# A two-block network on one core: a quarter of one MLP's up-projection matmuls walk their 512 columns in four other orders

## The chip, the cores and the metric

The kernel runs on one core of one Trainium2 chip. The metric is device time in microseconds of the whole program, from launch to end. The profile shows one execution of it, on five engines: TensorE (PE for matmuls, PEld for the loads of the stationary operand), VectorE (DVE), ScalarE (ACT), GpSimd (POOL) and SyncE (SP), beside the DMA queues.

## The reference, cut to what matters

The reference is a first block (a gated delta-net and retention mixer with a convolutional MLP) followed by a second block with two layers, each an attention and a relu-squared MLP. The change touches the MLP of the first of those two layers alone. Sizes: 512 tokens, model width 1024, hidden width 4096, all float32.

```python
def sq_relu_mlp(xn, w_in, w_out):
    h = jax.nn.relu(xn @ w_in)          # (512, 1024) @ (1024, 4096)
    return (h * h) @ w_out              # (512, 4096) @ (4096, 1024)

# in second_block, for i in range(2):
    h = h + mix
    h = h + sq_relu_mlp(rms_norm(h, norm_mlp_g[i]), mlp_w_in[i], mlp_w_out[i])
```

## The kernel before, in words

Everything is held feature-major: a tile has 128 features on the partitions and the 512 tokens as its columns. The normed activations of the MLP are eight such tiles, `st.x`, each as a pair: a rounded high part `xh` and the remainder `xl`, both of the type float32r (the trace prints their matmuls as f32). Weights come from HBM in the order of use, a block of 1024 x 256 at a time (line 243), and are split into `hi` and `lo` in the same way by ScalarE (line 251) and VectorE (line 252).

One output tile (128 hidden features x 512 tokens) is one call of `project` (line 381). It takes one bank of the accumulation memory (`ps`, 128 x 512 float32, tag `pj`, three buffers) and runs over the eight tiles of `st.x`; for each it issues three matmuls through `mm3` (line 190): hi by xh, hi by xl, lo by xh. So a tile of an up projection is 24 matmuls with 512 columns each, all adding into the same `ps`, each with its own load of 128 x 128 weights. All of them have line 188 in the profile (the helper `mm`), which is why they are told apart by their tiles: `ps_pj<-xh,hi`, `ps_pj<-xl,hi` and `ps_pj<-xh,lo`.

`mlp2(l, ...)` (line 962) is the relu-squared MLP of layer `l`. It goes through the hidden width in two halves. In each half a loop over eight weight blocks (`j`), two output tiles per block (`i`), calls `project`, then ScalarE takes relu out of `ps` into `s` (line 973), VectorE multiplies `ps` by `s` (line 974), and the product is split into `ah` (ScalarE, line 276) and `al` (VectorE, line 277). After sixteen tiles `out_proj` (line 440) multiplies them by the down weights: eight output tiles of 48 matmuls each, evacuated at lines 469 and 470. The order of the matmuls is the program's order; nothing is rescheduled by the change.

Elsewhere the kernel already reads and writes some tiles in other orders than the straight one, and the prediction uses these places:

- `cols_of` and `blocks` (lines 679 to 708): float32 matmuls whose moving operand is 64 columns in four runs of 16 (every other 16 of 128), written straight into `ps_X`, `ps_T` and `ps_U`.
- line 619: a matmul whose moving operand is two runs of 128 columns, 512 apart, written straight into `ps_gram`.
- `rev` (line 984): VectorE and ScalarE read `ps` backwards within each 128 columns, at lines 1383 and 1385 among others.
- `order`, `rorder` and `nat` (lines 1013 to 1028): for the second and third group of heads, line 1037 writes its output with a step of 128 or 32 elements between neighbours, and lines 1180 and 1252 read the accumulation memory in that way. For the first group, `order` is straight and `rorder` is `rev`.
- line 656: a VectorE copy out of a float32 tile with a step of 32 elements between neighbours.

## Time and profile before

| what | value |
|---|---|
| runs | 1921.4, 1927.18, 1923.35 us |
| median of the runs | 1923.35 us |
| the profiled execution, its own time | 1921.55 us |
| its span, first to last instruction | 1919.7 us |
| mean granted TensorE clock | 0.997 of full speed |
| busy | PE 98%, PEld 80%, DVE 58%, ACT 40%, POOL 7% |
| instructions on PE | 9219 matmuls, 9219 weight loads |
| chain that ended last, by engine | PE 55%, DVE 3%, ACT 1%, issue 1% |

[...] What a matmul costs in a stream is the distance from one start to the next, its pitch, and that is read from the timeline or from a long piece of the chain divided by its count.

### The profile page before, as it was taken

The page shows a single profiled execution, that of the slowest core. Times are in us where ns is not written, and L with a number is a line of the kernel's source. Part 1 is how long each engine was busy: PE and PEld are TensorE (multiplying, and loading weights), DVE is VectorE, ACT ScalarE, POOL GpSimd, SP SyncE. Part 2 cuts the span into 40 slices and gives each one's busy share as a digit, 9 for nine tenths or more (in the row PEclk, how much of TensorE's full clock was granted, in tenths as well). Part 3 has the DMA queues.
Part 4 walks back from the last instruction along what each step waited for, and adds up shares of the span by engine and source line. Part 5 has one row for each costly group of instructions (what it writes and reads, how often), then busy time and mean ns, then how long its engine had stood idle before and what let it go on. Part 6 is the DMA issues. An engine that isn't in the chain of part 4 may idle for free.

```text
span 1919.7 us, 23518 instructions
## 1 busy us (share of the span) xinstructions
PE 1885.3 (98%) x9219; PEld 1545.1 (80%) x9219; DVE 1109.8 (58%) x2109; ACT 766.1 (40%) x1350; POOL 143.3 (7%) x136
## 2 busy tenths in 40 slices
PE   7999999999999999999999999999999999999997
PEld 5887878788888887777888888888888888888886
DVE  7795756666356575558544344447877754334433
ACT  5523334343234444345342133336656543213322
POOL 1231210011001002000000000001111000000000
PEclk9999999999999999999999999999999999999999
DMA  5231213222322234112323222333222232222321
GB/s 191 79 116 56 74 45 121 95 88 88 110 103 86 76 112 160 64 52 99 110 89 109 88 106 92 111 131 135 95 73 101 81 112 88 97 101 89 109 88 44
DMA packets 39646, 185.53 MB, mean 97 GB/s; under 512 B 9055, under 2 KB 10847, under 8 KB 22000
## 3 DMA queue, kind: packets, MB, share of 16 engines
q1 hardware_dynamic: 37552, 177.45, 26.3%
q0 software_dynamic: 1984, 6.59, 1.0%
q8 instruction: 72, 1.18, 0.2%
q14 instruction: 38, 0.31, 0.1%
HBM read 176.31 MB, written 7.71 MB: 96 GB/s over the span
## 4 chain that ended last, share of the span: by engine, by line
PE 55%; DVE 3%; ACT 1%; issue 1%; DVEq 0%; ACTq 0%
PE ps_pj L188 49%; PE ps_ob L188 1%; PE ps_lgb L188 1%; PE ps_po L188 1%; PE ps_aT L1380 1%; PE ps_lg L188 1%; ACT junk L1397 0%; PE ps_bc L188 0%; DVE KL L1337 0%; DVE lo L252 0%; DVE nb L408 0%; DVE nb L409 0%; PE ps_obT L1409 0%; PE ps_pT L1140 0%; PE ps_mean L188 0%
## 5 line engine op out<-in xcount | busy, mean ns | idle before, releaser
L188 PE MATMUL ps_pj<-xh,hi 128*128 128x512 f32 x1504 | 592.2, 394 | 10.2 <-ACT hi L251 9.3
L188 PE MATMUL ps_pj<-xl,hi 128*128 128x512 f32 x1504 | 591.7, 393 | 0.0
L188 PE MATMUL ps_pj<-xh,lo 128*128 128x512 f32 x1504 | 590.9, 393 | 0.0
L251 ACT ACTIVATE hi<-raw 128x1024 fp32r<-128x1024 f32 (+2 forms) x308 | 317.2, 1031 | 649.1 <-PE ps_pj L188 611.0
L252 DVE TENSOR_TENSOR lo<-raw,hi 128x1024 fp32r<-128x1024 f32 (+2 forms) x308 | 369.6, 1202 | 300.2 <-ACT hi L251 299.2
L188 PEld LDWEIGHTS ps_pj<-xh,hi 128*128 128x128 f32 x1504 | 283.1, 188 | 69.0 <-ACT hi L251 9.8
L188 PEld LDWEIGHTS ps_pj<-xh,lo 128*128 128x128 f32 x1504 | 283.1, 188 | 58.1 <-DVE lo L252 1.1
L188 PEld LDWEIGHTS ps_pj<-xl,hi 128*128 128x128 f32 x1504 | 283.1, 188 | 57.6 <-DVE xl L280 0.6
L188 PE MATMUL ps_pj<-ah,lo 128*128 128x512 f32 (+1 forms) x704 | 271.0, 385 | 0.0
L188 PE MATMUL ps_pj<-al,hi 128*128 128x512 f32 (+1 forms) x704 | 270.7, 385 | 0.2 <-DVE al L277 0.2
L188 PE MATMUL ps_pj<-ah,hi 128*128 128x512 f32 (+1 forms) x704 | 270.9, 385 | 0.0
L188 PEld LDWEIGHTS ps_pj<-al,hi 128*128 128x128 f32 x704 | 132.3, 188 | 26.9 <-DVE al L277 0.5
L188 PEld LDWEIGHTS ps_pj<-ah,hi 128*128 128x128 f32 x704 | 132.3, 188 | 26.4 <-ACT ah L276 0.4
L188 PEld LDWEIGHTS ps_pj<-ah,lo 128*128 128x128 f32 x704 | 132.3, 188 | 25.9
L469 DVE TENSOR_TENSOR ot<-ps_pj,r 128x512 f32<-128x512 f32 x31 | 21.5, 692 | 108.1 <-PE ps_pj L188 108.1
L188 PE MATMUL ps_pj<-mh,hi 128*128 128x512 f32 x192 | 74.9, 394 | 1.0 <-ACT mh L276 0.9
L276 ACT ACTIVATE ah<-ms 128x512 fp32r<-128x512 f32 x64 | 40.4, 632 | 87.4 <-DVE ms L974 85.9
L188 PE MATMUL ps_pj<-ml,hi 128*128 128x512 f32 x192 | 74.4, 392 | 0.6 <-DVE ml L277 0.6
L188 PE MATMUL ps_pj<-mh,lo 128*128 128x512 f32 x192 | 74.0, 390 | 0.0
L277 DVE TENSOR_TENSOR al<-ms,ah 128x512 fp32r<-128x512 f32 x64 | 44.3, 693 | 45.0 <-ACT ah L276 45.0
L947 DVE SCALAR_TENSOR_TENSOR my<-ms,cols,my 128x511 f32<-128x511 f32 (+1 forms) x88 | 65.6, 748 | 2.8 <-ACT my L945 1.3
L1364 ACT ACTIVATE Lb<-Lb,bmn 128x512 f32<-128x512 f32 x64 | 45.6, 714 | 13.9 <-DVE bmn L1362 11.6
(341 smaller groups left out, 1895.9 us busy)
## 6 DMA issues: line engine op xcount, KB each, us to landing
raw<-w_all SPq DMA_DIRECT2D x137, 1024.0 KB
bt<-biasd SPq DMA_DIRECT2D x16, 448.0 KB
raw<-w_all SPq DMA_DIRECT2D x8, 768.0 KB
raw<-w_all SPq DMA_DIRECT2D x8, 640.0 KB
hscr<-h POOLq DMA_DIRECT2D x16, 256.0 KB, 2.5
hold<-hscr SPq DMA_DIRECT2D x16, 256.0 KB
hs<-x_t SPq DMA_DIRECT2D x8, 256.0 KB
hold<-x_t SPq DMA_DIRECT2D x8, 256.0 KB
```

The source lines that it names most:

```text
L188: return nc.tensor.matmul(o, lhsT=l, rhs=r, start=start, stop=stop)
L251: act(out=hv, in_=iv, func=AF.Copy)
L252: i_lo = V.tensor_tensor(out=lv, in0=iv, in1=hv.bitcast(F32), op=ALU.subtract)
L276: act(out=dst_hi, in_=src, func=AF.Copy)
L277: V.tensor_tensor(out=dst_lo, in0=src, in1=dst_hi.bitcast(F32), op=ALU.subtract)
L469: V.tensor_tensor(out=t, in0=ps, in1=scale_row, op=ALU.mult)
L947: V.scalar_tensor_tensor(out=y[:, jj:], in0=s[:, :T - jj], scalar=col(base + m), in1=y[:, jj:], op0=ALU.mult, op1=ALU.add)
L1364: act(out=L, in_=L, func=AF.Exp, scale=-1.0, bias=mn[:, j, t:t + 1], accum_out=ss[:, j, t:t + 1])
L1380: nc.tensor.transpose(ps[:, t * P:(t + 1) * P], A[t][:, kt * P:(kt + 1) * P], ident)
```

## The change

A table `VIEWS` names four pairs of weight blocks of the first relu-squared MLP (layer 0). For the tiles of these blocks `project` hands the matmul the same moving tiles and the same output tile, both seen through a view that lists the 512 columns in another order:

- half 0, blocks 2 and 3: columns 511 down to 0.
- half 0, blocks 6 and 7: 16 columns of the first 256, then 16 of the second 256, and so on (0 to 15, 256 to 271, 16 to 31, ...).
- half 1, blocks 2 and 3: the same with runs of 8.
- half 1, blocks 6 and 7: the same with runs of 2.

Moving operand and output use the same view, so each token's sum lands in the column where it landed before. Weights, order of the matmuls, their count and everything that reads `ps` afterwards stay as they are. Two blocks are four tiles, so each view covers 4 x 24 = 96 matmuls, 384 in all.

```diff
+VIEWS = {
+    (0, 0, 1): lambda ap: bass.AP(ap.tensor, ap.offset + T - 1, [list(ap.ap[0]), [-1, T]]),
+    (0, 0, 3): lambda ap: ap.rearrange("p (a i c) -> p i a c", a=2, c=16),
+    (0, 1, 1): lambda ap: ap.rearrange("p (a i c) -> p i a c", a=2, c=8),
+    (0, 1, 3): lambda ap: ap.rearrange("p (a i c) -> p i a c", a=2, c=2),
+}
@@ project
-    def project(pieces, x, n=T, cols=P):
+    def project(pieces, x, n=T, cols=P, view=None):
...
         nk = len(x)
+        if view is not None:
+            for k in range(nk):
+                hi, lo = pieces[k // KD]
+                M_["pe"] = mm3(view(ps), (hi[:, k % KD, 0:cols], lo[:, k % KD, 0:cols]),
+                               (view(x[k][0]), view(x[k][1])), k == 0, k == nk - 1)
+            return ps
@@ mlp2
-                        ps = project(w[i:i + 1], st.x)
+                        ps = project(w[i:i + 1], st.x, view=VIEWS.get((l, half, j // 2)))
```

## Rows read from the trace of the kernel before

**Rows 1.** The page: span, busy time by engine, granted clock in 40 slices.
```profile
span 1919.7 us, 23518 instructions
PE 1885.3 (98%) x9219; PEld 1545.1 (80%) x9219; DVE 1109.8 (58%) x2109; ACT 766.1 (40%) x1350; POOL 143.3 (7%) x136
PEclk9999999999999999999999999999999999999999
```
**Rows 2.** Chain that ended last, 940 to 1300 us: start, us, what.
```profile
944.06 1.16 PE ps_bc L188 x8
945.22 346.36 PE ps_pj L188 x1528
1291.58 0.95 PE ps_mean L188 x8
```
**Rows 3.** Stretches of the first relu-squared MLP: length, engines' busy (instructions), clock, DMA.
```profile
1030.00:1117.00 87.00, 87.00 (x386) 72.03 (x385) 30.47 (x33) 16.98 (x16) 0.00 (x0) 1.00 0.27 95
1117.00:1204.00 87.00, 87.00 (x386) 72.03 (x385) 39.72 (x48) 34.83 (x48) 0.00 (x0) 1.00 0.28 98
```
**Rows 4.** Waits, 943 to 1293 us: who waited for whom, us, times, longest.
```profile
ACT hi L251 <- PE ps_pj L188: 182.5, 62, 4.4
ACT ah L276 <- DVE ms L974: 43.7, 31, 1.4
```
**Rows 5.** Timeline of PE, one up tile with 512 columns: start, us, engine, line.
```profile
995.62 0.39 PE L188 MATMUL ps_pj<-xh,hi 128*128 128x512 f32 x1
...
1000.83 0.39 PE L188 MATMUL ps_pj<-xh,lo 128*128 128x512 f32 x1
```
**Rows 6.** Timeline of PE, last down tile, matmuls with 256 columns.
```profile
1895.77 0.28 PE L188 MATMUL ps_pj<-ah,hi 128*128 128x256 f32 x1
...
1898.65 0.28 PE L188 MATMUL ps_pj<-ah,hi 128*128 128x256 f32 x1
```
**Rows 7.** Groups by line and form: TensorE with two runs, with one, on 256 columns.
```profile
L188 PE MATMUL ps_gram<-KQ,kT x32: 379/379/564, 67.4 to 208.9; 128*128 128x256 f32 x32
L188 PE MATMUL ps_sT<-rqk 128*128 128x256 f32 x8 | 2.4, 379 | 0.0
```
**Rows 8.** Group (us, mean ns) and timeline: matmuls in runs of 16; of one column.
```profile
L188 PE MATMUL ps_X<-T,N 128*128 128x64 f32 x32 | 4.2, 275 | 0.7 <-POOL T L671 0.7
145.44 1.00 PE L188 MATMUL ps_X<-T,N 128*128 128x64 f32 x8
1291.51 1.02 PE L188 MATMUL ps_mean<-inv_d,acc 128*128 128x1 f32 x8
```
**Rows 9.** Other engines reading PSUM: straight, backwards, stepped (min/median/max or mean, ns).
```profile
L1443 DVE COPY bs<-ps_bias 16x512 f32<-16x512 f32 x3 | 2.0, 679 | 0.9 <-PE ps_bias L188 0.9
L1385 DVE COPY aT<-ps_aT 128x512 f32<-128x512 f32 x16 | 10.6, 683 | 0.8 <-PE ps_aT L1380 0.4 <-issue 0.2
L1180 DVE COPY L<-ps_bc x3: 681/681/694, 873.8 to 875.0; 128x512 f32<-128x512 f32 x3
L743 DVE COPY U<-ps_U 64x256 f32<-64x256 f32 x4 | 1.7, 417 | 4.6 <-PE ps_U L188 4.5
L430 ACT ACTIVATE rs<-ps_bc x5: 597/599/600, 30.6 to 1560.9; 128x512 f32<-128x512 f32 x5
L1252 ACT ACTIVATE oT<-ps_po x4: 598/598/599, 763.3 to 814.4; 128x512 f32<-128x512 f32 x4
L656 DVE COPY tt<-tt x2: 370/718/1066, 126.0 to 234.2; 64x256 f32<-64x256 f32 x2
```
**Rows 10.** Timeline of DVE, line 1037: backward, stepped, straight, stepped writes.
```profile
754.19 0.69 DVE L1037 TENSOR_TENSOR q<-ps_pj,rs 128x512 f32<-128x512 f32 x1 [1.60 <-PE ps_pj L188]
759.64 1.09 DVE L1037 TENSOR_TENSOR q<-ps_pj,rs 128x512 f32<-128x512 f32 x1 [4.75 <-PE ps_pj L188]
771.12 0.69 DVE L1037 TENSOR_TENSOR k<-ps_pj,rs 128x512 f32<-128x512 f32 x1 [6.69 <-PE ps_pj L188]
776.56 1.07 DVE L1037 TENSOR_TENSOR k<-ps_pj,rs 128x512 f32<-128x512 f32 x1 [4.75 <-PE ps_pj L188]
```

## The prediction

> **What bounds the kernel now.** I read the page first: TensorE is busy for 1885.3 of 1919.7 us and its granted clock stands at the top of the scale in all 40 slices [rows 1]. Then I looked for the place that the change touches, the first relu-squared MLP, in the chain of work that ended last. From 945.22 us on the chain is one unbroken piece of TensorE, 1528 matmuls in 346.36 us, which is 346.36 / 1528 = 226.7 ns per matmul [rows 2]; the MLP has 2 x (16 x 24 + 8 x 48) = 1536, so the piece is the whole of it but for the first few. The table by stretch says the same from the other side: in 87 us TensorE is busy for 87.00 us at a granted clock of 1.00, VectorE for 30 to 40 and ScalarE for 17 to 35 [rows 3]. The waits of that stretch are those of the others: ScalarE waited 182.5 us for TensorE to release weight buffers and 43.7 us for VectorE's squares [rows 4]; no wait of a matmul of the MLP is among them. So in this stage each nanosecond by which a matmul's pitch changes reaches the end of the program undiminished, and nothing else in the stage can give it back.

> **What a column costs.** The pitch has to be taken apart, because the change touches the columns only. With 512 columns 23 pitches take 1000.83 - 995.62 = 5.21 us, 226.5 ns each [rows 5]. The last down tile runs the same three products on 256 columns: 24 pitches in 1898.65 - 1895.77 = 2.88 us, 120.0 ns each [rows 6]. [...]

> **The change, part by part.** It removes and adds no instruction: 384 matmuls keep their place, their weights and their count of columns. No DMA, no wait and no queue moves. The readers of the output tile (relu on ScalarE, product on VectorE) read it straight as before, so their cost is nil on any account; if the matmuls of a tile became slower, those two would only wait longer for them, and the weight splits, which wait for TensorE now, have more time still. The one unknown is the pitch of 4 x 96 matmuls. Straight orders go to a new place in memory one column after the other. The new ones differ in two things: a step of -1, and jumps between the halves, 512 / 16 = 32, 512 / 8 = 64 and 512 / 2 = 256 of them per matmul.

> Jumps on TensorE: the trace has two kinds of matmul with a moving operand in pieces. Two runs of 128 take 379 ns, and a straight operand of 256 columns takes 379 ns too [rows 7]: one jump costs nothing that can be seen. Eight matmuls with four runs of 16 span 1.00 us, the last of them 275 ns, and eight with one column each 1.02 us [rows 8]; these are bound by their weight loads, so they say only that runs of 16 do no harm large enough to stick out behind those, (1.00 - 0.275) / 7, about 104 ns for 64 columns. That leaves room for half rate and more, so it does not prove the point at 0.416 ns per column.

> Backwards and stepped on the other engines: VectorE reads PSUM straight in 679 ns, backwards in 683, and with a step between all neighbours in no more than 694; ScalarE needs 599 straight and at most 599 stepped [rows 9]. A VectorE copy that reads SBUF with a step of 32 elements needs 370 ns for 256 elements in the better of its two records, while a straight one of 256 out of PSUM takes 417 [rows 9] (the other record, 1066, lies in a stage with much else going on). Writing SBUF backwards costs VectorE nothing either, 0.69 us against 0.69. Writing it with a step of 128 does: 1.09 us and 1.07 against 0.69 [rows 10], that is 0.40 us / 512 = 0.78 ns per element on top of (683 - 417) / 256 = 1.04 ns [rows 9], a factor of 1.75. This is the only row in which an order costs anything, and there every element jumps. In the change no column stands alone: each new order keeps neighbouring pairs together, the runs of 2 too.

> So the cost has these bounds. Below: the 13.5 ns per matmul could at the very most vanish, 384 x 13.5 = 5.2 us faster. Above, for one view: the stepped write's factor 1.75, which I round up to half rate: 512 x 0.416 = 213 ns per matmul, 96 x 213 = 20.4 us. For all four, 384 x 213 = 81.8 us. I take zero, because the reads in the trace are free in every order, and because the nearest TensorE row, the two runs, is free as well. Sum: 1921.55 us for the profiled execution, plus 0. The median of the runs shown lies 1.8 us above that execution; I put the forecast between the two, at **1922.5 us**. A measurement of this kernel can tell about 0.3%, 5.8 us, from no change.

> [...] No row here shows a matmul that writes its output out of order.

> **The rivals.**

> 1. The jumps cost, so that the time is longer: on the moving side each run opens a new place in SBUF, and the shorter the run, the less there is to hide that behind. A jump at VectorE's stepped-write price [rows 10] gives 32 x 0.78 = 25 ns, 64 x 0.78 = 50 ns and 256 x 0.78 = 200 ns per matmul; times 96: 2.4 + 4.8 + 19.2 = 26.4 us. At one column period per jump it is 1.3 + 2.6 + 10.2 = 14.1 us. If only the runs of 2 fall to half rate it is 20.4 us. So 1937 to 1949 us. It decides from 5.8 us / (96 x 352 jumps) = 0.17 ns per jump on. For it: TensorE asks for a run of 2 every 0.83 ns, faster than any engine in the trace, and stepped writes pay. Against it: stepped reads don't pay at one element per 1.04 ns, and the two runs didn't.

> 2. The backward order alone costs: if TensorE pairs neighbours only when they ascend, its 96 matmuls fall to half rate, +20.4 us, 1943 us. For it: 0.416 ns per column is 2.5 times VectorE's rate, so something may handle two at once. Against it: backward reads and writes at 683 and 0.69, as straight [rows 9, 10].

> 3. Every order that isn't one ascending run halves the rate, on the output side: +81.8 us, 2004 us. For it: nothing in the trace, which has no such output. Against it: the runs of 16 are 32 straight pieces, and reads of PSUM in any order are free [rows 9]. [...]

> 4. The change does not do what it says: a view in two dimensions could be issued as two matmuls of 256 columns. Then the pitch is 2 x 120.0 = 240 instead of 226.5, and even on all 384 that is 5.2 us, inside what can't be told from no change; the count of matmuls would show it.

> [...]

> **How the numbers follow.** No cost: 0.57. Split into two: 0.02. Jumps cost: 0.20. Backwards alone: 0.10. All at half rate: 0.09. Faster: 0.02. So within 0.3%: 0.57 + 0.02 = 0.59; slower: 0.20 + 0.10 + 0.09 = 0.39; faster: 0.02. The range reaches from 1918, the forecast less most of what the fixed part could give, to 1949, the upper end of the first rival, and takes in the second. It leaves out the third, and with it about 1 in 10.

> **What the profile of the changed kernel would show.** If I am right, the chain still has one TensorE piece of about 346 us there, and the timeline shows a pitch of 226 to 227 ns in all four places: about 961 to 983 us (backwards), 1005 to 1027 (runs of 16), 1135 to 1157 (runs of 8) and 1179 to 1201 (runs of 2). Under the first rival the pitch rises from one view to the next with the count of runs, with the runs of 2 at 330 to 440 ns; under the second only the first place changes, to 440 ns; under the third all four read about 440. A tile's span in the first place, 24 pitches, tells it at a glance: 5.4 us or 10.5 (24 x 0.4395). If all four pitches stay and the time still moves, the step that failed is that nothing else is touched.

## The result: 0.7% slower, and the whole of it in the pitch of the four places

| | before | changed |
|---|---|---|
| median of 6 runs | 1923.34 us | 1936.98 us |
| lowest to highest | 1921.4 to 1929.89 | 1935.74 to 1944.41 |
| ratio, 95% interval | | 1.0069 [1.0049, 1.0089] |
| the profiled execution, span | 1919.7 us | 1940.9 us |

The forecast was no change, 1922.5 us; the time lies 14.5 us above it, inside the range but clearly on the slower side. The page of the changed kernel and the piece of its chain that answers to [rows 2] (start, us, what):

```profile
span 1940.9 us, 23528 instructions
PE 1904.6 (98%) x9219; PEld 1549.8 (80%) x9219; DVE 1109.5 (57%) x2109; ACT 766.1 (39%) x1350; POOL 143.4 (7%) x136
...
950.81 1.16 PE ps_bc L197 x8
951.97 360.85 PE ps_pj L197 x1528
1312.83 0.88 PE ps_mean L197 x8
```

The piece has the same 1528 matmuls as in [rows 2] and takes 360.85 us in place of 346.36: 14.49 us more, which is the loss of the medians (13.6 us) to within a microsecond. It begins 6.75 us later than before, 951.97 against 945.22, and that has nothing to do with the change, whose matmuls come after this point. In 150 to 200 us, in the mixer, this execution had a granted clock of 0.83 where the other had 0.97; single runs of both kernels are longer by some 6 us at a lower mean clock (1942.7 us at 0.994 against 1936.97 at 0.997 in the changed one, 1928.16 at 0.994 against 1922.47 at 0.997 in the one before, measured beside `e3_without_2`). The stretch in the changed kernel, then in the one before (columns as in [rows 3]):

```profile
150.00:200.00 50.00, 47.46 (x336) 37.97 (x336) 25.06 (x90) 14.12 (x50) 4.34 (x5) 0.83 0.14 52
```

```profile
150.00:200.00 50.00, 47.45 (x361) 38.36 (x361) 28.20 (x98) 18.41 (x65) 7.97 (x8) 0.97 0.14 53
```

The timeline of TensorE in the four places, each time a matmul and the 24th after it (so their starts are 24 pitches apart; compare [rows 5]): backwards, runs of 16, of 8 and of 2.

```profile
969.79 0.40 PE L197 MATMUL ps_pj<-xh,hi 128*128 128x512 f32 x1
...
975.39 0.40 PE L197 MATMUL ps_pj<-xh,hi 128*128 128x512 f32 x1
...
1014.75 0.40 PE L197 MATMUL ps_pj<-xh,hi 128*128 128x512 f32 x1
...
1020.51 0.40 PE L197 MATMUL ps_pj<-xh,hi 128*128 128x512 f32 x1
...
1149.60 0.41 PE L197 MATMUL ps_pj<-xh,hi 128*128 128x512 f32 x1
...
1155.44 0.41 PE L197 MATMUL ps_pj<-xh,hi 128*128 128x512 f32 x1
...
1194.65 0.51 PE L197 MATMUL ps_pj<-xh,lo 128*128 128x512 f32 x1
...
1202.81 0.51 PE L197 MATMUL ps_pj<-xh,lo 128*128 128x512 f32 x1
```

24 pitches take 5.60, 5.76, 5.84 and 8.16 us: 233.3, 240.0, 243.3 and 340.0 ns, against 226.7 straight. The excesses, 6.7, 13.3, 16.6 and 113.3 ns, times 96 are 0.6, 1.3, 1.6 and 10.9 us, together 14.4: the whole loss. All four places cost something, and the runs of 2 cost three quarters of it. In every experiment below a pitch is read in this way, over the middle 88 of the 96 matmuls of a pair of blocks (over the last 57 for the first pair of an MLP, in which the norm's matmuls fall).

### The profile page after: what moved, and what is told of

Its sections match the earlier page's. It is cut to its first block, busy times and chain, and to the rows that moved or that the text cites. A ratio compares the mean times of both kernels' runs of the same rounds, so it can differ in the third digit from the quotient of the medians.

```text
span 1940.9 us, 23528 instructions
## 1 busy us (share of the span) xinstructions
PE 1904.6 (98%) x9219; PEld 1549.8 (80%) x9219; DVE 1109.5 (57%) x2109; ACT 766.1 (39%) x1350; POOL 143.4 (7%) x136
## 4 chain that ended last, share of the span: by engine, by line
PE 55%; DVE 3%; ACT 1%; issue 1%; DVEq 0%; ACTq 0%
PE ps_pj L197 49%; PE ps_ob L197 1%; PE ps_lgb L197 1%; PE ps_po L197 1%; PE ps_aT L1395 1%; PE ps_lg L197 1%; ACT junk L1412 0%; DVE lo L261 0%; PE ps_bc L197 0%; DVE KL L1352 0%; DVE nb L423 0%; DVE nb L424 0%; PE ps_obT L1424 0%; PE ps_pT L1155 0%; PE ps_mean L197 0%
## 5 line engine op out<-in xcount | busy, mean ns | idle before, releaser
L197 PE MATMUL ps_pj<-xh,hi 128*128 128x512 f32 x1504 | 598.5, 398 | 12.0 <-ACT hi L260 11.0
L197 PE MATMUL ps_pj<-xh,lo 128*128 128x512 f32 x1504 | 597.0, 397 | 0.0
L261 DVE TENSOR_TENSOR lo<-raw,hi 128x1024 fp32r<-128x1024 f32 (+2 forms) x308 | 369.5, 1201 | 316.3 <-ACT hi L260 315.3
```

The costliest lines, as they stand in the source:

```text
L197: return nc.tensor.matmul(o, lhsT=l, rhs=r, start=start, stop=stop)
L261: i_lo = V.tensor_tensor(out=lv, in0=iv, in1=hv.bitcast(F32), op=ALU.subtract)
```

## The experiments

### Which part of the change costs what

Without the runs of 2 (`e3_without_2`), and with them alone (`e4_only_2`):

```diff
 VIEWS = {                       # e3_without_2
     (0, 0, 1): ..., (0, 0, 3): ..., (0, 1, 1): ...,
-    (0, 1, 3): lambda ap: ap.rearrange("p (a i c) -> p i a c", a=2, c=2),
 }
 VIEWS = {                       # e4_only_2
-    (0, 0, 1): ..., (0, 0, 3): ..., (0, 1, 1): ...,
     (0, 1, 3): lambda ap: ap.rearrange("p (a i c) -> p i a c", a=2, c=2),
 }
```

> The change without its runs of 2. By the pitches in the changed kernel's trace the rest is 96 x (6.7 + 13.3 + 16.5) ns = 3.5 us over before, a ratio of 1.002; if all of the loss were elsewhere in the program, 1.007 would stay.

> The runs of 2 alone: 96 x 113.4 ns = 10.9 us over before, a ratio of 1.0057, and the two excesses of this and the kernel without them add up to that of the whole change, 14.4 us. If the loss were elsewhere, the ratio would not split like this.

Measured: ratios 1.0011 [0.9990, 1.0033] and 1.0040 [1.0018, 1.0061] to before, which add up to 1.0051, inside the interval of the whole change. The runs of a kernel on that chip spread over some 17 us, so the piece of the chain is the sharper witness. It holds the same 1528 matmuls in each kernel; first without the runs of 2, then with them alone:

```profile
951.68 349.98 PE ps_pj L196 x1528
```

```profile
951.62 357.26 PE ps_pj L194 x1528
```

Over the 346.36 us of [rows 2] these are 3.62 and 10.90 us, and their sum, 14.52, is the 14.49 of the whole change. The parts don't act on one another.

### Which side pays: the reads or the adding writes

Each pair of blocks of both relu-squared MLPs gets a view of its own, for the moving operand (first) and for the output (second):

```diff
+def walk(off, *dims):           # dims: (step, count), outermost first
+    return lambda ap: bass.AP(ap.tensor, ap.offset + off, [list(ap.ap[0])] + [list(d) for d in dims])
+def turns(c):                   # halves in turn by runs of c
+    return walk(0, (c, 256 // c), (256, 2), (1, c))
+def plain(c):                   # straight, in the same three dimensions
+    return walk(0, (2 * c, 256 // c), (c, 2), (1, c))
+BACK = walk(T - 1, (-1, T))     # same(ap) gives ap back
+    (0, 0, 1): (BACK, same), (0, 0, 2): (same, BACK),
+    (0, 1, 3): (turns(2), plain(2)), (1, 0, 0): (plain(2), turns(2)),
...
-                M_["pe"] = mm3(view(ps), ..., (view(x[k][0]), view(x[k][1])), ...)
+                vx, vp = view
+                M_["pe"] = mm3(vp(ps), ..., (vx(x[k][0]), vx(x[k][1])), ...)
```

> All sixteen pairs of up-projection blocks (both layers) get a view of their own, and what is read is the pitch of 24 matmuls in each. Some views sit on the moving operand alone or on the output alone, the other side straight; there the columns of the sums are mixed up, so those tiles don't hold the reference's values. The changed kernel showed 226.7 ns straight, 233.3 backwards, 240.0 in runs of 16, 243.2 in runs of 8 and 340.0 in runs of 2. Theory R, the moving operand's reads pay: read alone gives 233, 240, 243 and 340, output alone 226.7 in all four. Theory W, the output's writes pay: the other way round. Theory J, each jump costs a step of the address stream on whichever side: both sides alone give the full pitch. Views on both sides: runs of 4 between 243 and 340, near 280; 32, 64 and 128 by one column period per jump (16, 8, 4 jumps) 233, 230, 228; straight written as 32 runs of 16, 226.7 if jumps count and 240 if runs count. Runs of 2 that step on by 4 columns (0, 1, 4, 5, ...) 340 if each run pays. The whole run about 1923 + 96 x 0.45 = 1966 us.

The second kernel, `e2_walks`, has other orders in the same places, such as

```diff
+    (0, 0, 1): (walk(2, (4, 128), (-2, 2), (1, 2)),) * 2,    # 2, 3, 0, 1, 6, 7, 4, 5, ...
+    (1, 1, 3): (walk(1, (2, 256), (-1, 2)),) * 2,            # 1, 0, 3, 2, ...
+    (0, 1, 2): (walk(0, (2, 16), (32, 16), (1, 2)),) * 2,    # pairs, 32 columns between neighbours
```

> Again a view for each pair of blocks; where the two sides differ, the tiles don't hold the reference's values. Pairs swapped within each four columns (2, 3, 0, 1, 6, 7, ...), so that 256 runs of 2 stay within their four columns: if each new run pays, 340 ns; if it is the coming back to the same four columns that pays, 226.7 to 233. Read alone and output alone tell the side. Runs of 2 that step by 32 or 128 columns between neighbours: 340 if each run pays whatever the distance. Runs of 16 taken from the last to the first: 240 if each jump pays, less if only the distance of 256 columns does. Runs of 16 each walked backwards: 233 or more. Runs of 4 and of 32 on one side alone: by theory R (reads pay) the read side has all, by W (writes pay) the output. Neighbours swapped (1, 0, 3, 2, ...): 340 by theory J (each jump), 233 if it is like backwards. Straight written as runs of 2: 226.7. The whole run 1950 to 1975 us.

Pitches measured, in ns (226.7 is straight):

| order | both sides | moving operand alone | output alone |
|---|---|---|---|
| straight, written in two or three dimensions | 226.7 | | |
| backwards | 233.3 | 233.3 | 226.7 |
| halves in turn, runs of 128; 64 | 226.7; 226.7 | | |
| halves in turn, runs of 32 | 236.6 | 236.6 | 226.7 |
| halves in turn, runs of 16 | 240.0 | 240.0 | 226.7 |
| halves in turn, runs of 8 | 243.3 | 243.3 | 226.7 |
| halves in turn, runs of 4 | 250.0 | 250.0 | 226.7 |
| halves in turn, runs of 2 | 340.0 (333.3 in the other layer) | 340.0 | 226.7 |
| pairs, steps of 4 (0, 1, 4, 5, ...) | 453.4 | 453.3 | 226.7 |
| pairs, 32; 128 columns between neighbours | 453.3; 443.3 | | |
| pairs swapped within four (2, 3, 0, 1, ...) | 226.7 | 226.7 | 226.7 |
| neighbours swapped (1, 0, 3, 2, ...) | 226.7 | | |
| runs of 16 from last to first | 233.3 | 233.3 | |
| runs of 16, each walked backwards | 266.7 | | |

The two timelines that decide it, 24 pitches each: runs of 2 on the moving operand alone, then on the output alone.

```profile
1189.56 0.51 PE L228 MATMUL ps_pj<-xh,lo 128*128 128x512 f32 x1
...
1197.72 0.51 PE L228 MATMUL ps_pj<-xh,lo 128*128 128x512 f32 x1
...
1579.83 0.39 PE L228 MATMUL ps_pj<-xh,lo 128*128 128x512 f32 x1
...
1585.27 0.39 PE L228 MATMUL ps_pj<-xh,lo 128*128 128x512 f32 x1
```

8.16 us against 5.44. Theory R holds in every pair that was measured on one side: the reads have the whole cost, and the output may be written backwards, in halves by turns, in pairs with steps of 4 or by swapped pairs for nothing. The times of the two runs agree with the pitches: the excesses of `e1_sides` add up to 533 ns, times 96 is 51.2 us, on 1922 gives 1973; measured 1973.15. For `e2_walks` 756 ns, 72.6 us, 1995; measured 1995.54. (The kernel before takes 1922 to 1924 us on that chip at the same mean clock, 0.997.) Both lie above what I had expected, 1966 and 1950 to 1975 us, mainly because pairs in steps cost more than the 340 ns that I had given them.

Several of my expectations fell, and two of them led on. The cost is not one price per jump: 256 swaps within four columns are free (226.7), while 256 steps by pairs that never come back cost 226.7 ns, twice the 113.3 of the change's 256 jumps over 256 columns. And runs of 64 and of 128 columns cost nothing (226.7), so the cost doesn't go by the count of jumps.

### What the reads pay for

The moving operand alone, with orders that read some columns twice:

```diff
+    (0, 0, 0): (walk(0, (0, 128), (1, 4)), ...),             # the same four columns
+    (0, 0, 3): (walk(0, (0, 128), (256, 2), (1, 2)), ...),   # two fixed pairs in turn
+    (1, 0, 1): (walk(0, (0, 4), (4, 128)), ...),             # every fourth column, four times
```

> Views on the moving operand alone, the output straight; some read columns twice and leave others out, so these tiles don't hold the reference's values. It tells apart what is paid for. Theory G: each visit to another group of 4 columns (16 bytes of float32) takes about 4 column periods of 0.417 ns, and further columns of the group just visited are free until then. Theory J: each break of the ascending order is paid, wherever it goes. Pitches expected, straight 226.7: the same group of 4 again and again, G 226.7, J 250 or more (128 breaks). The same pair again and again (256 breaks), G 226.7, J 340. Two neighbouring groups in turn by pairs, and two groups 256 columns apart (256 visits, 256 breaks each): 453 if the last group alone is kept, 226.7 if two are kept, 340 as in the change if something between. Four groups in turn, near or 128 columns apart: 453 by G. Runs of 4 that straddle two groups: 340 to 453 by G, 250 by J; the same runs on the groups' bounds: 250 by both. Every second column (256 visits, 2 breaks): 453 by G, 227 by J if a step is no break. Every fourth (512 visits): 867 to 907 by G. Pairs that straddle two groups, ascending: 453 by both; pairs on the bounds, ascending: 453. Every second run of 4, of 8, of 16, ascending (128 visits): 227 to 250. Groups from the last to the first, each ascending: 233 to 250. The whole run about 2020 to 2040 us.

Measured: the same four columns 215.8, the same two 215.8; two groups in turn by pairs, neighbours 216.7, 256 columns apart 217.8; four neighbouring groups in turn 437.2; runs of 4 across the bounds of groups 330.0 (over the last 57, because its first six took 1210.05 - 1207.50 = 2.55 us, 425 ns each, after the order before had ended at a granted clock of 0.50), on the bounds 243.3; every second column 451.1; pairs ascending, on the bounds 451.1, across them 453.3; every second run of 4, 8 and 16: 231.1, 233.3 and 240.0; groups from last to first 233.3. Four groups 128 columns apart took 571.2, where 453 was expected. The granted clock fell during them from 1.00 to 0.50, but their first six pitches, at 1.00, are no shorter, 573 ns (see the last section), so this is what the order costs. The kernel took 2074 us, more than the 2020 to 2040 expected.

Theory J is out: 256 breaks within one pair cost nothing (215.8). Theory G has the groups of four right and the price wrong. Every fourth column, 512 visits to groups, should have taken 867 to 907 ns. Its timeline, 24 pitches:

```profile
1669.77 0.64 PE L228 MATMUL ps_pj<-xh,lo 128*128 128x512 f32 x1
...
1680.84 0.65 PE L228 MATMUL ps_pj<-xh,lo 128*128 128x512 f32 x1
```

11.07 / 24 = 461.3 ns, hardly more than pairs with half as many visits. And a new fact: reading the same group over and over is faster than reading straight, 215.8 against 226.7.

So a third theory, S, which goes by the order alone: the columns at its even places and those at its odd places count apart. Straight, the even places take 0 and 2 out of a group, then 4 and 6 out of the next: two in a row, and 226.7 ns. In pairs with steps of 4 (453.3), and in every fourth column (461.3), they take one from each. S says that the pitch is the straight one where the even and the odd places each take two or more in a row from a group, and twice that where they take one. The test is to leave the groups' visits alone and change only how the even and the odd places share them (`e7_streams`, moving operand alone unless noted):

```diff
+    (0, 1, 0): (walk(0, (0, 2), (2, 128), (256, 2)), ...),   # 0, 256, 2, 258, ...
+    (0, 1, 1): (walk(0, (0, 2), (1, 128), (256, 2)), ...),   # 0, 256, 1, 257, ...
+    (0, 1, 2): (walk(0, (0, 4), (4, 64), (256, 2)), ...),    # 0, 256, 4, 260, ...
+    (0, 0, 2): (walk(0, (8, 64), (1, 4), (4, 2)), ...),      # 0, 4, 1, 5, 2, 6, 3, 7, ...
```

> Views mostly on the moving operand alone, the output straight (its sums are then in other columns or read columns twice, so these tiles don't hold the reference's values). Every fourth column had cost 461 ns for 512 visits to groups of 4, no more than pairs with 256 visits (453), so the visit to a group is not the unit. Theory S: the columns at even and at odd places of the order are read by two streams, each of which needs two columns in a row from one group of 4, or halves its rate. Theory B: one stream of pairs, each pair needs its group to be the one at hand. Single columns of the two halves in turn, every second column (0, 256, 2, 258, ...): S 226.7, as each stream takes two from a group; B 340 to 453. Runs of 1 (0, 256, 1, 257, ...): S 226.7, B 340 to 453. Columns 0, 256, 4, 260, ...: S 453, B 453 or more. 0, 4, 4, 8, 8, 12, ...: S 453; B 340 or less. Within four 0, 2, 1, 3: both 226.7. Within eight 0, 4, 1, 5, 2, 6, 3, 7 and within sixteen 0, 8, 1, 9, ...: S 226.7, B 340. Two places 160 columns apart in turn by pairs, walking up: 340 as with 256 by both. Pairs 0, 1, 4, 5, 2, 3, 6, 7, 4, 5, ...: 340. Eight neighbouring groups in turn by pairs: 440. Four groups in turn by pairs, 32, 64 and 132 columns apart: 440 as for neighbours if the 571 ns at 128 apart came of that distance alone. Even groups and then odd ones, every second run of 8, and the upper half before the lower, on both sides: 227 to 235. The whole run about 2030 us.

| order | in a row from a group, at even and at odd places | S said | B said | measured |
|---|---|---|---|---|
| 0, 256, 2, 258, ... | two | 226.7 | 340 to 453 | 226.7 |
| 0, 256, 1, 257, ... | four | 226.7 | 340 to 453 | 215.8 |
| 0, 4, 1, 5, 2, 6, 3, 7, ... | four | 226.7 | 340 | 215.8 |
| 0, 8, 1, 9, ... within 16 | four | 226.7 | 340 | 215.8 |
| 0, 2, 1, 3, ... within 4 | two | 226.7 | 226.7 | 226.7 |
| 0, 256, 4, 260, ... | one | 453 | 453 | 453.3 |
| 0, 4, 4, 8, 8, 12, ... | one | 453 | 340 or less | 453.3 |

The timelines of the first, the second and the sixth of these, 24 pitches each:

```profile
1144.79 0.39 PE L228 MATMUL ps_pj<-xl,hi 128*128 128x512 f32 x1
...
1150.23 0.39 PE L228 MATMUL ps_pj<-xl,hi 128*128 128x512 f32 x1
...
1164.65 0.38 PE L228 MATMUL ps_pj<-xh,lo 128*128 128x512 f32 x1
...
1169.83 0.38 PE L228 MATMUL ps_pj<-xh,lo 128*128 128x512 f32 x1
...
1189.52 0.63 PE L228 MATMUL ps_pj<-xl,hi 128*128 128x512 f32 x1
...
1200.40 0.63 PE L228 MATMUL ps_pj<-xl,hi 128*128 128x512 f32 x1
```

5.44, 5.18 and 10.88 us: 226.7, 215.8 and 453.3 ns. Theory S gets each of the seven right or errs on the side of a gain; theory B fails in five. The rest of that kernel, which took 2080.44 us, some 50 more than expected: two places 160 columns apart in turn by pairs 328.3, where I had said 340; eight neighbouring groups in turn 473.3, where I had said 440; four groups in turn 482.3 at 32 columns apart, 573.3 at 64 and 436.6 at 132, so the 571.2 at 128 did not come of that one distance alone; on both sides, even groups and then odd 231.1, every second run of 8 232.4, upper half before lower 226.7 (over the last 57; its first six took 1933.65 - 1931.10 = 2.55 us, 425 ns each, after a place with a granted clock of 0.55); and pairs 0, 1, 4, 5, 2, 3, 6, 7, 4, ... 218.3, where I had said 340.

**What stays open.** In that last one, 218.3, and in two fixed pairs in turn, 217.8, the even places go to and fro between two groups, one column from each, and so do the odd ones, and it costs nothing; in the change's runs of 2 they do so too, but both groups are new after every four pairs, and then it costs 113 ns, half of the 226.7 that pairs in steps of 4 cost. Theory S as it stands puts all three at twice the straight pitch, and with them the two places 160 columns apart (328.3) and the runs of 4 across the bounds (330.0). So of the runs of 2, three quarters of the change's loss, it gives the kind of cost and not the size. S is an account of which orders cost what; the two streams of which the expectation of `e7_streams` speaks are my guess, and no trace shows them. Nor do these runs settle the smaller prices of runs of 4 to 32 and of backward walks (4.4 to 40.0 ns), whose even and odd places have two in a row, nor why four groups in turn cost more at 64 and 128 columns apart than at 132.

### Other orders that cost nothing

The change once more, both sides, with orders that leave two in a row from a group of four to the even places and to the odd ones:

```diff
+    (0, 0, 1): walk(2, (4, 128), (-2, 2), (1, 2)),                           # 2, 3, 0, 1, ...
+    (0, 0, 3): walk(1, (2, 256), (-1, 2)),                                   # 1, 0, 3, 2, ...
+    (0, 1, 1): lambda ap: ap.rearrange("p (a i c) -> p i a c", a=2, c=64),
+    (0, 1, 3): lambda ap: ap.rearrange("p (a i c) -> p i a c", a=2, c=128),
```

> The change with four other orders, both sides: pairs swapped within each four columns (256 runs of 2), neighbours swapped (1, 0, 3, 2, ...), halves in turn by runs of 64 and by runs of 128. By theory G each visits every group of 4 once and nearly in order: all four pitches 226.7, the time as before, ratio 1.000. If it is the order as such, or the number of runs, that costs, it is slower by 10 to 20 us, as with the change.

Measured: ratio 1.0005 [0.9984, 1.0026], and the piece of the chain is the straight one's, 346.38 us:

```profile
947.39 346.38 PE ps_pj L201 x1528
```

### A kernel that is faster than both

The orders with four in a row at the even places and at the odd ones took 215.8 ns, 10.9 less than straight. To use that, the tokens must lie so that reading 0, 256, 1, 257, ... gives them in order, while the output stays straight. The splits, which write the moving tiles, store them so:

```diff
+    def odd_even(ap):
+        return ap.rearrange("p (a b) -> p b a", a=2)
+    def straight(ap):
+        return ap.rearrange("p (b a) -> p b a", a=2)
-    def mm3(ps, w, x, first, last):
+    def mm3(ps, w, x, first, last, hf=None):
...
         (wh_, wl_), (xh_, xl_) = w, x
+        ps = straight(ps)
+        if hf is None:              # hf: halves of 256 columns, in the last down tile
+            xh_, xl_ = odd_even(xh_), odd_even(xl_)
...
     def split(dst_hi, dst_lo, src, scale=None):
+        dst_hi, dst_lo, src = odd_even(dst_hi), odd_even(dst_lo), straight(src)
```

> Not the change but what the experiments point to: the order 0, 256, 1, 257, ... gave a pitch of 215.7 ns where straight has 226.7. Every moving tile of float32r (the normed x, the hidden activations, the mixers' outputs) is stored by its split with the even tokens in columns 0 to 255 and the odd ones in 256 to 511, and every three-product matmul reads it 0, 256, 1, 257, ..., so that the tokens arrive in order and the output is written straight. Theory S (two streams, four columns in a row from each group): about 7100 matmuls of 512 columns by 11 ns, 78 us less, 1845 us; ScalarE's and VectorE's splits, which now write with a jump at each element, may take up to 1.1 us instead of 0.7 each, and where the last split before a projection is waited for that costs some 6 x 1 us: 1845 to 1855. If the gain in pitch came only of reading other data in that experiment, the time is 1923 or more.

Measured: 1901.49 us, ratio 0.9861 [0.9830, 0.9892]. Only some 27 us of the expected 78 arrive. The groups of TensorE show a part of where the rest went: it now waits 18.2 us for the splits of ah and mh (last columns: idle before, and for whom), which in the kernel before were 0.0 us for ah and 1.0 for mh.

```profile
L188 PE MATMUL ps_pj<-ah,hi 128*128 128x512 f32 (+1 forms) x704 | 265.6, 377 | 12.0 <-ACT ah L291 12.0
L188 PE MATMUL ps_pj<-mh,hi 128*128 128x512 f32 x192 | 73.8, 388 | 6.2 <-ACT mh L291 5.1 <-ACT mh L294 1.0
```

In the first MLP, 345 to 700 us, TensorE was busy for 354.78 of 355 us before and for 339.66 now, and its granted clock was 0.98 there in place of 1.00 (columns as in [rows 3]; before, then now):

```profile
345.00:700.00 355.00, 354.78 (x1559) 291.70 (x1558) 208.86 (x272) 136.16 (x183) 28.38 (x22) 1.00 0.27 94
```

```profile
345.00:700.00 355.00, 339.66 (x1548) 291.70 (x1547) 212.89 (x277) 142.14 (x178) 29.06 (x24) 0.98 0.27 93
```

So the next kernel keeps that MLP's activations and the mixers' outputs straight, and stores only the normed x and the relu-squared activations apart:

```diff
-        split(xh, xl, src, wcol)
-        st.x.append((xh, xl))
+        split(xh, xl, src, wcol, True)
+        st.x.append((xh, xl, True))
...
-                        split(hi, lo, s)
-                        acts.append((hi, lo))
+                        split(hi, lo, s, None, True)
+                        acts.append((hi, lo, True))
```

> Even tokens in columns 0 to 255 and odd ones in 256 to 511, read 0, 256, 1, 257, ..., only for the normed x (48 tiles) and the hidden activations of the two relu-squared MLPs; the first MLP's activations and the mixers' outputs, whose splits TensorE waited for in the kernel that stores all tiles so (12.0 us for ah, 6.2 for mh), are stored and read straight. About 6100 matmuls by 10.9 ns, 66 us less, against splits that take 0.4 to 0.5 us longer on two engines where a projection waits for x. If those waits were what ate 78 us down to about 27, this one is faster than that kernel: 1875 to 1895 us where before has 1923. If the loss came with the normed x, no better than 1.4% under before.

Measured: 1876.79 us against 1928.09 on the same chip, ratio **0.9729 [0.9699, 0.9759]**. Its page, and the pieces of its chain in the two relu-squared MLPs:

```profile
span 1873.2 us, 23565 instructions
PE 1826.8 (98%) x9219; PEld 1554.0 (83%) x9219; DVE 1152.0 (62%) x2109; ACT 814.8 (43%) x1350; POOL 142.8 (8%) x136
...
933.10 325.92 PE ps_pj L188 x1510
1530.15 256.41 PE ps_pj L188 x1188
```

325.92 / 1510 and 256.41 / 1188 are both 215.8 ns, against 226.7 [rows 2]. TensorE's busy time fell by 1885.3 - 1826.8 = 58.5 us, its idle time rose from 34.4 to 46.4, most of what the 51 us lack to the 66. The price lies on the two engines that split, in groups by form (us, mean ns), before and then now:

```profile
L276 ACT ACTIVATE ah<-ms 128x512 fp32r<-128x512 f32 x64 | 40.4, 632 | 87.4 <-DVE ms L974 85.9 <-issue 1.5
L277 DVE TENSOR_TENSOR al<-ms,ah 128x512 fp32r<-128x512 f32 x64 | 44.3, 693 | 45.0 <-ACT ah L276 45.0
```

```profile
L293 ACT ACTIVATE ah<-ms 128x512 fp32r<-128x512 f32 x64 | 71.5, 1116 | 87.2 <-DVE ms L991 85.8 <-issue 1.5
L294 DVE TENSOR_TENSOR al<-ms,ah 128x512 fp32r<-128x512 f32 x64 | 71.0, 1109 | 76.3 <-ACT ah L293 76.3
```

632 and 693 ns have become 1116 and 1109: a stepped write as in [rows 10], on ScalarE as on VectorE, and these engines have the time there.

## Why the prediction was wrong

- **Where the time is bound: right.** Each nanosecond of pitch came out at the end: 14.4 us worked out from four pitches, 14.49 in the chain, 13.6 in the medians. Nothing else in the stage moved. (The piece of [rows 2] is not quite what I took it for: it lacks the first 26 matmuls of this MLP and has the first 18 of the next attention at its end, at the same pitch.)
- **"I take zero, because the reads in the trace are free in every order": the step that failed.** Those reads were VectorE's and ScalarE's, VectorE's at (683 - 417) / 256 = 1.04 ns per element and ScalarE's at 599 ns for 512 [rows 9]; for TensorE 256 columns more took 226.5 - 120.0 = 106.5 ns, 0.416 per column [rows 5, 6]. Of the orders that read each column once, those with no cost (226.7) all had two or more in a row from a group of four columns at their even and at their odd places, and even that was no promise (backwards 233.3). The four orders of the change cost 6.7, 13.3, 16.6 and 113.3 ns in place of zero, all of it in the reads of the moving operand. The prediction saw the difference in rate and put it under the first rival, but let the slow engines' rows decide. The TensorE row that it leaned on, two runs of 128 [rows 7], was right and said nothing about short runs: runs of 64 and of 128 are free here too, at 226.7. The bound that mattered was left as not proven [rows 8].
- **The 13.5 ns beside the columns: they depend on the order.** They are what two pitches leave if a matmul costs a fixed part and a part per column, 226.5 - 512 x 0.416 = 13.5 [rows 5, 6]; that split is my estimate, and no run shows that 0.416 ns is the least a column can take, on which their use as the bound below rested. In place of 13.5 the runs showed 215.8 - 213.0 = 2.8 ns with four in a row at the even and at the odd places, so the straight order itself pays 11 ns per matmul for its reads; what the 11 ns are, no run here shows. 11 of the 13.5 ns could be had, 4.2 us on 384 matmuls and within the 5.2 us that the prediction named as the very most, only not in the four orders of the change.
- **The first rival: its sum right, its mechanism wrong.** 0.416 ns per jump gave 14.1 us, and 14.4 were measured. That is luck, for the single terms were 1.3, 2.6 and 10.2 for runs of 16, 8 and 2 and 0 backwards, against 1.3, 1.6, 10.9 and 0.6, and 256 jumps within groups of four cost nothing: there is no price per jump. That the shorter runs would cost more, and the runs of 2 most of all, was right.
- **The second rival** (backwards at half rate) fell: 6.7 ns, not 213. **The third** (any order on the output side halves the rate) fell altogether: output alone 226.7 in eight orders, all of which keep pairs side by side; a matmul that writes single columns apart was not run.
- **The fourth** (split into two) fell: 9219 matmuls on the page, as before.
- **The chances** had slower at 0.39, with the first rival at 0.20. The range held the time because it took that rival's bounds in.

## What to carry to other kernels

That TensorE takes a straight column in 0.416 ns [rows 5, 6] tells nothing of how much slack its reads have, and free reads on VectorE at 1.04 ns per element [rows 9] are no evidence for it: the orders of the change cost TensorE up to 113.3 ns per matmul. For float32r matmuls of this kind the output cost nothing in each of the eight orders tried (226.7), all of which keep pairs together, and the moving operand is what to lay out with care: in `e7_streams` four in a row from one group of four, at the even places of the order and at the odd ones, took 215.8 ns, two 226.7 and one 453.3. Where the engine that writes the operand has time to spare, storing it for that order saves 11 of 227 ns per matmul, and the place to stop is where the writer's longer instruction (1116 and 1109 ns in place of 632 and 693) is waited for, 18.2 us in `e8_odd_even`.

## What the runs showed of the hardware that was not expected

```profile
1152.66 0.75 PE L228 MATMUL ps_pj<-xh,hi 128*128 128x512 f32 x1
...
1156.10 0.76 PE L228 MATMUL ps_pj<-xh,hi 128*128 128x512 f32 x1
```

```profile
1111.00:1152.00 41.00, 41.00 (x95) 19.38 (x94) 9.90 (x12) 7.17 (x10) 0.00 (x0) 1.00 0.14 52
1152.70:1156.10 3.40, 3.40 (x8) 1.25 (x6) 1.83 (x2) 2.00 (x3) 0.00 (x0) 1.00 0.15 19
1156.30:1206.00 49.70, 49.70 (x88) 27.83 (x88) 8.16 (x10) 6.72 (x9) 0.00 (x0) 0.50 0.11 40
```
